# An encoder layer on one core: raw tiles of y in the weight ring, the pooling gate in the attention branch's loop, and the last combinations behind the last token tile's norm

## The chip, the cores and the metric

The kernel runs on one core of one Trainium2 chip. The metric is the device time of one execution, in microseconds (us). The core's engines run side by side, each with its own queue in program order: TensorE (PE) for matmuls and transposes, VectorE (DVE) for arithmetic on tiles, ScalarE (ACT) for activations, copies and casts, GpSimd (POOL) for a part of the arithmetic, and SyncE (SP), which issues most of the transfers (DMAs). They wait for one another through semaphores. Tiles lie in SBUF, 128 partitions of 128 rows or columns, and matmul results in eight banks of PSUM.

## The reference

One layer (DEPTH = 1) of an encoder over 1024 tokens with 1024 channels, in float32:

```python
h = rmsnorm(x, g_mix[l])
z = h @ w_in[l]
...
y_pool = pool_mixer(u_pool, w_pool_grp[l], pool_scale[l])
...
y_attn = diff_attention(q, k, v, g_q[l], g_k[l], lam, g_sub[l], lambda_init)

gates = jax.nn.sigmoid(h @ w_gate[l] + b_gate[l])
merged = (gates[..., :D_MODEL] * (y_pool @ w_branch_pool[l])
          + gates[..., D_MODEL:] * (y_attn @ w_branch_attn[l]))
x = x + merged @ w_out[l]

h2 = rmsnorm(x, g_ffn[l])
x = x + jnp.square(jax.nn.relu(h2 @ w_up[l])) @ w_down[l]
```

`y_attn` ends in a norm per head: a scale per token and head, and a gain `g_sub` per channel. `w_branch_pool` is 512 x 1024, `w_branch_attn` and `w_out` 1024 x 1024, `w_up` 1024 x 4096 and `w_down` 4096 x 1024.

## The kernel before

*How numbers are held.* Each float32 operand of a product is split in a high part (a cast, on ScalarE) and a low part (the difference, on VectorE or GpSimd): `split` (L115). A product is three matmuls, high by high, high by low and low by high: `mm3` (L120, the matmuls at L123 to L125).

*Stages.* After the norm, the projections, the pooling mixer, the attention and the gate products `g` (whose sums are kept in DRAM as `g_dram`), the stages around the change are these, in the order in which TensorE runs them:

1. *Pooling branch* `bp` (`branch_pool` L215, called in the loop L795 to L801). Eight groups `d` of 128 output channels, two halves of 512 tokens each, 12 matmuls per half. `gate` (L204) loads the pooling gate's sums into two tiles `gp` and takes their sigmoid; L220 multiplies the product out of its PSUM bank by it into `mp`. The same loop prepares the attention branch's other operand: `load_split` (L188) loads a raw tile of `y` (128 channels by 1024 tokens, `ryT`), loads the head's scales `rb` as a broadcast row, multiplies the two with the gain (L196), and splits the result into `yT`. The raw tiles come from `raw` (L109), a pool of N_RAW = 2 buffers, which the raw weights use too.
2. *Attention branch* `ba` (loop L803 to L814). For each of the eight groups, `load_cols` (L148) loads a raw tile `rba` of `w_branch_attn` and splits it into two tiles `wba`; a gate tile `ga` is loaded; two halves of 24 matmuls follow; L810 multiplies the bank by `ga`, GpSimd adds `mp` (L811), and the sum is split into `mT`.
3. *Output projection* `op` (`out_proj`), with the residual added on VectorE into the token tile `y[t]`, for eight token tiles of 128 tokens.
4. *Second norm* (`norm_token` L887): the sum of squares `nsq` on ScalarE, the mean and a power on VectorE and GpSimd (`rsq`, the power at L246), the scale on ScalarE (L898), the gain `gfb` on VectorE (L901), eight transposes on TensorE (L904, `hb`). Tokens 4 to 7 go through `second_half` (L959), which makes the operands T1 and T2 of a Strassen-Winograd product; `combine` (L972) makes T3, 22 and T4 of them, and splits T1.
5. *Up projection* (`up_pair` L1012): `w_up` in 16 pairs of column blocks, seven products of 12 matmuls per pair, on operands of the weights (`A`, and the sums S1 to S4, split into `AS`) and of the tokens (B11, B21, T1, T2, T3, 22, T4). The products are gathered in banks called X, Y, Z and W: X takes the first, sixth and seventh product in turn, and its content is copied out by ScalarE in between (x1 L1028, U2 L1055, U3 L1064).
6. *Down projection*, with banks `Da` and `Db`.

*What sets the order.* The tile framework takes the program, orders the instructions of each engine by priority and by what is ready, and puts in the waits. `tc.cur_priority` is set by hand where something is to come earlier or later. A tile of a pool can be written again only when all readers of its former content are done. So the number of buffers of a pool sets how far ahead a load can go. Split weights come out of the ring `wt` (L129): eight slots called W, then four called fw, counted in turn. Small tiles of 512 columns come from `tmp` (two `fr` and two `fo` tiles, in turn).

In the up projection the two lists that the change touches are these. `up_pair` is a generator: its first stretch, up to the first `yield`, makes products 1 and 2, which need only B11 and B21; the second issues a load; the rest makes the other five. The loop at L1091 runs `second_half` for tokens 4 to 7 with priorities of the output projection; the loop at L1096 then advances pairs 0 to 3 and calls `combine` for T1, T3, 22 and T4.

Of the kernel before, what the change touches and what calls it, by code (L numbers as in the profile page):

```python
# [17 lines left out]
P = 128  # L18
# [37 lines left out]
def encoder_kernel(  # L56
# [52 lines left out]
    def raw(shape, name):  # L109
        return rpool.tile(shape, F32, tag="raw", name=name)  # L110

    def f(ap):
        return ap.bitcast(F32)

    def split(hi, lo, src, lo_eng=None):  # L115

        nc.scalar.copy(hi, src)  # L117
        (lo_eng or nc.vector).tensor_tensor(lo, src, f(hi), op=ALU.subtract)  # L118

# [8 lines left out]

    def wt(shape, name):  # L129

        wcount[0] += 1
        if wcount[0] > N_QKVW and (wcount[0] - N_QKVW - 1) % (N_W + N_FW) >= N_W:
            return fw_tile(shape, name)
        return wpool.tile(shape, F32R, tag="W", name=name, bufs=N_W)

    def fw_tile(shape, name):
        return wpool.tile(shape, F32R, tag="fw", name=name, bufs=N_FW)

# [6 lines left out]
    def fu_tile(name):  # L145
        return fq.tile([P, S], F32, tag="fu", name=name)
# [42 lines left out]
    def load_split(src, r0, name, tile_fn, scale=None):  # L189

        rw = raw([P, S], f"r{name}")
        nc.sync.dma_start(rw, src[r0 : r0 + P, :])
        if scale is not None:
            rb, row = scale
            nc.sync.dma_start(rb, row.partition_broadcast(P))
            nc.vector.scalar_tensor_tensor(rw, rw, gs, rb, op0=ALU.mult, op1=ALU.mult)  # L196
        ts = []
        for th in range(2):
            t = tile_fn([P, 2, 512], F32R, f"{name}_{th}", th)
            split(t[:, 0, :], t[:, 1, :], rw[:, th * 512 : (th + 1) * 512])  # L200
            ts.append(t)
        return ts
# [11 lines left out]

    def branch_pool(d, ws, gts, gp, ps_fn):  # L215
        gate(gts, d)
        m = htile([P, S], F32, f"mp{d}", 1)
        for th in range(2):
            ps = proj_T(ps_fn(f"bp{d}_{th}"), ws, lambda k, th: pair(ypT[k][th]), th, nk=4)
            nc.vector.tensor_tensor(m[:, th * 512 : (th + 1) * 512], ps, gp[th], op=ALU.mult)  # L220
        mp.append(m)
# [570 lines left out]
    ypT = [load_split(p_dram, g * P, f"ypT{g}", ypt_tile) for g in range(4)]  # L792
    mp, yT = [], []
    for d in range(NK):
        if d % 2 == 0 and d + 2 < NK:  # L795
            ws_bp[d + 2] = load_cols2(w_branch_pool, (d + 2) * P, f"bp{d + 2}")
        gp = [tmp(f"gp{d}_{th}") for th in range(2)]
        branch_pool(d, ws_bp[d - d % 2][d % 2], [(gp[0], 0, 512), (gp[1], 512, S)], gp, bank)
        rb = fu_tile(f"rb{d}") if d % 2 else ut([P, S], F32, f"rb{d}")
        yT.append(load_split(y_dram, d * P, f"yT{d}", yt_tile(d), (rb, r_dram[d])))  # L800
    mT = {}  # L801
    for d in range(NK):
        ws = load_cols(w_branch_attn, d * P, f"ba{d}")  # L803
        ga = fu_tile(f"ga{d}") if d % 2 else ut([P, S], F32, f"ga{d}")
# [26 lines left out]
    def sub(eng, out_, a, b):  # L831
# [7 lines left out]
    pr2 = [pool_of(hs, "pr20", 1, side="right")]  # L839
    py = pool_of(norms, "py", 4, side="right")  # L840
    nt = pool_of(norms, "nt", 1, side="right")
    Bq = {
        q: tuple(nb_pool.tile([P, 4, 512], F32R, tag="h", name=f"B{q}{i}") for i in "hl")
# [7 lines left out]
    def out_proj(ws, t, dh):  # L851
        th, c0 = t // 4, (t % 4) * P
        cs = slice(dh * 512, (dh + 1) * 512)
        if t not in y:
            y[t] = py.tile([P, D], F32, tag="y", name=f"y{t}")
        nc.sync.dma_start(y[t][:, cs], x[t * P : (t + 1) * P, cs])
# [26 lines left out]
    def b_split(q, c0, src, eng):  # L883
        hi, lo = Bq[q]
        split(hi[:, :, c0 : c0 + P], lo[:, :, c0 : c0 + P], src, eng)

    def norm_token(t, bank_fn):  # L887
# [9 lines left out]
        rsq(rs, rs, 1, 1.0)  # L897
        nc.scalar.activation(yn, yn, AF.Copy, scale=rs)  # L898
        for j, b in enumerate(ps):
# [57 lines left out]
    kept_b = {}  # L957
    T1s = {}

    def second_half(t):  # L960
# [3 lines left out]
        nc.sync.dma_start(t1, nd[0, t - 4])  # L964
        b12, b22 = norm_token(t, lambda j, name: bm.tile([P, 512], F32, tag="ZWY"[j], name=name))
        sub(dve, t1, b12, t1)
# [3 lines left out]
        nc.scalar.copy(kept_b[t][:, 1], b22)  # L970
        b_split("T2", c0, t2, dve)

# [42 lines left out]
    def up_pair(p):  # L1015
# [23 lines left out]
        def store(name, src, queue=nc.sync):  # L1039
# [7 lines left out]
        S1, S2, S3, S4 = (  # L1047
            (e2 if p % 3 or i > 2 else es).tile([P, 4, P], F32, tag="sm", name=f"s{i}_{p}")
            for i in range(1, 5)
# [38 lines left out]
    pairs = [up_pair(p) for p in range(NP)]  # L1088
    now = tc.cur_priority
    for t in range(4, NT):  # L1090
        tc.cur_priority = prio[min(t + 1, NT - 1)]  # L1091
        second_half(t)
    tc.cur_priority = now
    AHEAD = 4
    for p, q in zip(range(AHEAD), ("T1", "T3", "22", "T4")):
        next(pairs[p])  # L1096
        if q == "T1":
            next(pairs[0])
        if q == "T3":
            body = tc.cur_priority  # L1100
        combine(q)
    norms.close()
    e2 = pool_of(hs, "e2", N_E2, side="right")
    pr2.append(pool_of(hs, "pr21", N_R2 - 1, side="right"))
    now, tc.cur_priority = tc.cur_priority, body
    for _ in pairs[0]:
# [184 lines left out]
```

## Time and profile before

| what | before |
|---|---|
| median of 3 runs | 1564.49 us (1564.31 to 1566.15) |
| profiled execution, its own time | 1563.08 us |
| span of that execution in the profile | 1561.3 us |
| mean granted clock of TensorE | 0.997 of full speed |
| instructions in the profile | 22059, of them 7649 matmuls and transposes |

The page of the profile gives, for one execution, the busy time of each engine, the chain of work that ended last, and the costliest groups of instructions. A group's row names the line, the engine, the operation and its output and inputs by the program's names. The list of waits names, for an engine, the tile that it waited to use, the engine, tile and line that released it, the total in us, how often, and the longest. A row of the order of time has the start in us, the length in us, the engine and line, the operation, and in brackets the idle time before it with what ended it; "xN" joins N like instructions that follow one another. A row of a view by tile has the shortest, median and longest duration in ns, and the first and last start. A row of a stretch has its length, then the busy time and the number of instructions of PE, its weight loads, DVE, ACT and POOL, the granted clock of TensorE (1.00 is full speed), the DMA engines' busy share and GB/s.

### The profile page before, as it was taken

How to read it: one execution, taken by the hardware profiler on the slowest of the kernel's cores; microseconds unless marked ns; L12 is line 12 of the kernel's file. 1: busy time of each engine (PE TensorE's matmuls, PEld its weight loads, DVE VectorE, ACT ScalarE, POOL GpSimd, SP SyncE). 2: the span in 40 equal slices, each digit the busy share in tenths (PEclk: the TensorE clock that was granted, in tenths of full speed). 3: DMA queues.
4: the chain of work that ended last, by engine and by line, in shares of the span. 5: the costliest groups of instructions: out<-in, count | busy, mean ns of one | idle time of the engine just before them, and what ended most of it. 6: DMA issues, size and time to landing. Idle time of an engine off the chain costs nothing.

```text
span 1561.3 us, 22059 instructions
## 1 busy us (share of the span) xinstructions
PE 1537.9 (99%) x7649; PEld 1323.7 (85%) x7649; DVE 1007.5 (65%) x2273; ACT 809.2 (52%) x1792; POOL 353.3 (23%) x447
## 2 busy tenths in 40 slices
PE   7999999999999999999899999999999999999999
PEld 6999999999999989888788887888888788888887
DVE  7777677777878797645222458766666668556662
ACT  6656656656565655554422556555555634333331
POOL 6433333343434252221644400000000000000000
PEclk9999999999999999999999999999999999999999
DMA  7111212121212021248526634555342789537750
GB/s 228 51 52 48 64 46 63 32 66 49 63 41 70 31 92 42 69 148 283 180 92 184 207 108 121 175 168 177 132 138 108 255 309 382 199 122 248 227 192 27
DMA packets 166393, 206.41 MB, mean 132 GB/s; under 512 B 10037, under 2 KB 102922, under 8 KB 166282
## 3 DMA queue, kind: packets, MB, share of 16 engines
q1 hardware_dynamic: 148874, 177.71, 35.0%
q10 hardware_dynamic: 17408, 27.30, 4.7%
q8 instruction: 60, 0.98, 0.3%
q14 instruction: 51, 0.42, 0.1%
HBM read 150.42 MB, written 54.56 MB: 131 GB/s over the span
## 4 chain that ended last, share of the span: by engine, by line
PE 87%; DVE 4%; DMA 4%; ACT 1%; POOL 1%; issue 1%; SPq 1%; POOLq 0%; DVEq 0%; ACTq 0%
PE z L123 5%; PE z L125 5%; PE z L124 5%; PE Da L124 4%; PE Da L123 4%; PE Da L125 4%; PE g L124 3%; PE g L123 3%; PE g L125 3%; PE Db L124 3%; PE Db L123 3%; PE Db L125 3%; PE X L123 3%; PE X L124 3%; PE X L125 3%; PE sc L496 2%
## 5 line engine op out<-in xcount | busy, mean ns | idle before, releaser
L123 PE MATMUL z<-wqkv,hT 128*128 128x384 f32 x512 | 174.7, 342 | 0.4 <-DVE qn L438 0.3
L125 PE MATMUL z<-wqkv,hT 128*128 128x384 f32 x512 | 174.3, 341 | 0.3 <-DVE hT L118 0.2
L124 PE MATMUL z<-wqkv,hT 128*128 128x384 f32 x512 | 173.6, 339 | 0.0
L507 ACT ACTIVATE s<-s,nm 128x256 f32<-128x256 f32 (+7 forms) x128 | 99.6, 778 | 48.7 <-DVE nm L499 43.3
L246 POOL TENSOR_TENSOR ms<-ms,mhalf 128x4 f32<-128x4 f32 x64 | 66.5, 1040 | 157.6 <-DVE ms L245 139.0
L125 PE MATMUL g<-hT,fwgate 128*128 128x512 f32 x256 | 101.0, 394 | 0.0
L124 PE MATMUL g<-hT,fwgate 128*128 128x512 f32 x256 | 100.9, 394 | 0.0
L123 PE MATMUL g<-hT,fwgate 128*128 128x512 f32 x256 | 100.9, 395 | 0.0
L123 PEld LDWEIGHTS z<-wqkv,hT 128*128 128x128 f32 x512 | 96.8, 189 | 4.3 <-DVE qn L438 1.2
L124 PEld LDWEIGHTS z<-wqkv,hT 128*128 128x128 f32 x512 | 96.8, 189 | 2.9
L125 PEld LDWEIGHTS z<-wqkv,hT 128*128 128x128 f32 x512 | 96.6, 189 | 2.9 <-DVE hT L118 1.3
L499 DVE CUSTOM_DVE_ANT_0 s<-sc,dist 128x512 f32<-128x512 f32 (+3 forms) x128 | 74.7, 586 | 22.1 <-PE sc L497 20.7
L118 POOL TENSOR_TENSOR wqkv<-rqkv,wqkv 128x384 fp32r<-128x384 f32 x60 | 63.8, 1080 | 20.2 <-ACT wqkv L117 18.3
L118 DVE TENSOR_TENSOR AS<-s,AS 128x512 fp32r<-128x512 f32 x64 | 43.9, 688 | 36.9 <-ACT AS L117 36.6
L496 PE MATMUL sc<-K,Q 128*128 128x512 f32 (+2 forms) x192 | 67.2, 355 | 0.1
L497 PE MATMUL sc<-K,Q 128*128 128x512 f32 (+2 forms) x192 | 66.5, 354 | 0.0
L444 POOL TENSOR_TENSOR qn<-qn,ggh 128x128 f32<-128x128 f32 x64 | 32.9, 514 | 137.5 <-DVE qn L438 119.3
L470 ACT CAST Q<-tk 64x128 fp32r<-64x128 f32 x128 | 33.2, 259 | 58.3 <-DVE Q L469 56.5
L467 ACT CAST Q<-tk 64x128 fp32r<-64x128 f32 x128 | 33.1, 258 | 50.5 <-DVE K L466 49.1
L118 POOL TENSOR_TENSOR fwgate<-frgate,fwgate 128x512 fp32r<-128x512 f32 x32 | 45.1, 1412 | 51.9 <-ACT fwgate L117 51.7
L125 PEld LDWEIGHTS g<-hT,fwgate 128*128 128x128 f32 x256 | 48.1, 188 | 8.6
L123 PE MATMUL ba<-yT,wba 128*128 128x512 f32 x128 | 51.2, 400 | 3.9 <-ACT wba L117 3.9
(428 smaller groups left out, 4638.5 us busy)
## 6 DMA issues: line engine op xcount, KB each, us to landing
wd<-in_w_down_dram SPq DMA_DIRECT2D x56, 512.0 KB, 5.8
wu<-in_w_up_dram SPq DMA_DIRECT2D x32, 512.0 KB, 4.5
udS<-us SPq DMA_DIRECT2D x64, 256.0 KB, 2.2
ur<-udS SPq DMA_DIRECT2D x32, 512.0 KB, 3.4
rqkv<-in_w_in_dram SPq DMA_DIRECT2D x64, 192.0 KB, 2.8
ud<-u ACTq DMA_DIRECT2D x48, 256.0 KB, 2.5
ur<-ud SPq DMA_DIRECT2D x24, 512.0 KB, 4.3
frgate<-in_w_gate_dram SPq DMA_DIRECT2D x32, 256.0 KB, 2.9
```

Of the source, the lines that this page charges most:

```text
L118: (lo_eng or nc.vector).tensor_tensor(lo, src, f(hi), op=ALU.subtract)
L123: nc.tensor.matmul(ps, lhs_hi, rhs_hi, start=first, stop=False, **kw)
L124: nc.tensor.matmul(ps, lhs_hi, rhs_lo, start=False, stop=False, **kw)
L125: nc.tensor.matmul(ps, lhs_lo, rhs_hi, start=False, stop=last, **kw)
L246: nc.gpsimd.tensor_tensor(dst, dst, mhalf[:, :n], op=ALU.pow)
L444: nc.gpsimd.tensor_tensor(qn[:, 2:4, :], qn[:, 2:4, :], ggh.unsqueeze(1).broadcast_to([P, 2, HD]), op=ALU.mult)
L467: nc.scalar.copy(q_hi, q)
L470: nc.scalar.copy(Q[other, m, 1, :], q)
L496: nc.tensor.matmul(dst, Q[:, i, 0, :], rhs, start=True, stop=False)
L497: nc.tensor.matmul(dst, Q[:, i, 1, :], rhs, start=False, stop=True)
L499: nc.vector.tensor_tensor_reduce(out=s[i][:, c : c + w], in0=sc[:, 0:w], in1=dist[:, o0 + c : o0 + c + w], scale=2.0 ** -(h + 1), scalar=B ...
L507: nc.scalar.activation(s[i][:, 0:n], s[i][:, 0:n], AF.Exp, bias=last, scale=-1.0, accum_out=Z[:, i, t : t + 1])
```

## The change

The change has these parts.

- `load_split` takes the raw tile from the weight ring `wt`, in F32, where a scale is given (the tiles of `y`); `wt` and `fw_tile` take a type for it. The scales come as a list of tiles: one of 1024 columns as before, or two of 512 from `tmp`, with a load and a multiplication each. Two of every four groups use the halves.
- `branch_pool` no longer loads the gate and no longer multiplies: ScalarE copies the bank into `mp`. The gate's load, sigmoid and multiplication, now in place on `mp`, go into the attention branch's loop.
- The attention branch's weights are loaded ahead: groups 0, 1 and 2 in the pooling loop at d = 5, 6, 7, and group d + 2 at the head of each turn of the attention loop. Group 2 is loaded in both.
- The token tiles `y` come from four pools of one tile each in place of one pool of four, and the pool `nt` is made before them. The pool `e2` of six tiles becomes `e20` (two) and `e21` (four): pair 0 and the pairs divisible by three use `es` and `e20`, pair 1 too, and the others `e21`.
- For the last token tile the second half's sum of squares uses bank Z in place of Y. Pair 0's first two stretches and pair 1's first are advanced before the last token tile's `second_half`, at a priority 100 later than what was reached.
- `combine` of T3, 22 and T4 is put behind the scale of token tile 7 (`issue_after`: what is emitted in that context is not ordered ahead of that instruction), and T4 also behind the split of that tile's T2. `split` and `b_split` return their last instruction for this, and `norm_token` keeps the scale in `scaled`.

```diff
--- before.py
+++ after.py
@@ -115,7 +115,7 @@
     def split(hi, lo, src, lo_eng=None):
 
         nc.scalar.copy(hi, src)
-        (lo_eng or nc.vector).tensor_tensor(lo, src, f(hi), op=ALU.subtract)
+        return (lo_eng or nc.vector).tensor_tensor(lo, src, f(hi), op=ALU.subtract)
 
     def mm3(ps, lhs_hi, lhs_lo, rhs_hi, rhs_lo, first, last, more=False):
 
@@ -126,15 +126,15 @@
 
     wcount = [0]
 
-    def wt(shape, name):
+    def wt(shape, name, dt=F32R):
 
         wcount[0] += 1
         if wcount[0] > N_QKVW and (wcount[0] - N_QKVW - 1) % (N_W + N_FW) >= N_W:
-            return fw_tile(shape, name)
-        return wpool.tile(shape, F32R, tag="W", name=name, bufs=N_W)
-
-    def fw_tile(shape, name):
-        return wpool.tile(shape, F32R, tag="fw", name=name, bufs=N_FW)
+            return fw_tile(shape, name, dt)
+        return wpool.tile(shape, dt, tag="W", name=name, bufs=N_W)
+
+    def fw_tile(shape, name, dt=F32R):
+        return wpool.tile(shape, dt, tag="fw", name=name, bufs=N_FW)
 
     def fo_tile(name):
         return fp.tile([P, 528], F32, tag="fo", name=name, bufs=N_FO)
@@ -188,12 +188,15 @@
 
     def load_split(src, r0, name, tile_fn, scale=None):
 
-        rw = raw([P, S], f"r{name}")
+        rw = raw([P, S], f"r{name}") if scale is None else wt([P, S], f"r{name}", F32)
         nc.sync.dma_start(rw, src[r0 : r0 + P, :])
         if scale is not None:
-            rb, row = scale
-            nc.sync.dma_start(rb, row.partition_broadcast(P))
-            nc.vector.scalar_tensor_tensor(rw, rw, gs, rb, op0=ALU.mult, op1=ALU.mult)
+            rbs, row = scale
+            n = S // len(rbs)
+            for i, rb in enumerate(rbs):
+                js = slice(i * n, (i + 1) * n)
+                nc.sync.dma_start(rb, row[js].partition_broadcast(P))
+                nc.vector.scalar_tensor_tensor(rw[:, js], rw[:, js], gs, rb, op0=ALU.mult, op1=ALU.mult)
         ts = []
         for th in range(2):
             t = tile_fn([P, 2, 512], F32R, f"{name}_{th}", th)
@@ -212,12 +215,12 @@
     def pair(t):
         return t[:, 0, :], t[:, 1, :]
 
-    def branch_pool(d, ws, gts, gp, ps_fn):
-        gate(gts, d)
+    def branch_pool(d, ws, ps_fn):
+
         m = htile([P, S], F32, f"mp{d}", 1)
         for th in range(2):
             ps = proj_T(ps_fn(f"bp{d}_{th}"), ws, lambda k, th: pair(ypT[k][th]), th, nk=4)
-            nc.vector.tensor_tensor(m[:, th * 512 : (th + 1) * 512], ps, gp[th], op=ALU.mult)
+            nc.scalar.copy(m[:, th * 512 : (th + 1) * 512], ps)
         mp.append(m)
 
 
@@ -790,17 +793,30 @@
 
     ws_bp = {0: load_cols2(w_branch_pool, 0, "bp0")}
     ypT = [load_split(p_dram, g * P, f"ypT{g}", ypt_tile) for g in range(4)]
-    mp, yT = [], []
+    mp, yT, ws_ba = [], [], {}
+
     for d in range(NK):
         if d % 2 == 0 and d + 2 < NK:
             ws_bp[d + 2] = load_cols2(w_branch_pool, (d + 2) * P, f"bp{d + 2}")
-        gp = [tmp(f"gp{d}_{th}") for th in range(2)]
-        branch_pool(d, ws_bp[d - d % 2][d % 2], [(gp[0], 0, 512), (gp[1], 512, S)], gp, bank)
-        rb = fu_tile(f"rb{d}") if d % 2 else ut([P, S], F32, f"rb{d}")
+        elif d > NK - 4:
+            j = len(ws_ba)
+            ws_ba[j] = load_cols(w_branch_attn, j * P, f"ba{j}")
+        branch_pool(d, ws_bp[d - d % 2][d % 2], bank)
+        if d % 4 < 2:
+            rb = [fu_tile(f"rb{d}") if d % 2 else ut([P, S], F32, f"rb{d}")]
+        else:
+            rb = [tmp(f"rb{d}_{i}") for i in range(2)]
         yT.append(load_split(y_dram, d * P, f"yT{d}", yt_tile(d), (rb, r_dram[d])))
     mT = {}
     for d in range(NK):
-        ws = load_cols(w_branch_attn, d * P, f"ba{d}")
+        if d + 2 < NK:
+            ws_ba[d + 2] = load_cols(w_branch_attn, (d + 2) * P, f"ba{d + 2}")
+        ws = ws_ba.pop(d)
+        gp = [tmp(f"gp{d}_{th}") for th in range(2)]
+        gate([(gp[0], 0, 512), (gp[1], 512, S)], d)
+        for th in range(2):
+            mh = mp[d][:, th * 512 : (th + 1) * 512]
+            nc.vector.tensor_tensor(mh, mh, gp[th], op=ALU.mult)
         ga = fu_tile(f"ga{d}") if d % 2 else ut([P, S], F32, f"ga{d}")
         gate(whole(ga)[0], NK + d)
         for th in range(2):
@@ -837,8 +853,8 @@
     nb_pool = pool_of(hs, "nb", 4, side="right")
     pr1 = pool_of(hs, "pr1", N_R1, side="right")
     pr2 = [pool_of(hs, "pr20", 1, side="right")]
-    py = pool_of(norms, "py", 4, side="right")
     nt = pool_of(norms, "nt", 1, side="right")
+    py = [pool_of(norms, f"py{i}", 1, side="right") for i in range(4)]
     Bq = {
         q: tuple(nb_pool.tile([P, 4, 512], F32R, tag="h", name=f"B{q}{i}") for i in "hl")
         for q in ("11", "21")
@@ -852,7 +868,7 @@
         th, c0 = t // 4, (t % 4) * P
         cs = slice(dh * 512, (dh + 1) * 512)
         if t not in y:
-            y[t] = py.tile([P, D], F32, tag="y", name=f"y{t}")
+            y[t] = py[t % 4].tile([P, D], F32, tag="y", name=f"y{t}")
         nc.sync.dma_start(y[t][:, cs], x[t * P : (t + 1) * P, cs])
         if th:
             ps = pb.tile([P, 512], F32, tag="b", name=f"op{t}_{dh}")
@@ -882,7 +898,9 @@
 
     def b_split(q, c0, src, eng):
         hi, lo = Bq[q]
-        split(hi[:, :, c0 : c0 + P], lo[:, :, c0 : c0 + P], src, eng)
+        return split(hi[:, :, c0 : c0 + P], lo[:, :, c0 : c0 + P], src, eng)
+
+    scaled = {}
 
     def norm_token(t, bank_fn):
 
@@ -895,7 +913,7 @@
         ps = [bank_fn(j, f"hb{t}_{j}") for j in range(2)]
         nc.vector.tensor_scalar(rs, ss[:, 0:1], ss[:, 1:2], 1.0 / D, op0=ALU.add, op1=ALU.mult)
         rsq(rs, rs, 1, 1.0)
-        nc.scalar.activation(yn, yn, AF.Copy, scale=rs)
+        scaled[t] = nc.scalar.activation(yn, yn, AF.Copy, scale=rs)
         for j, b in enumerate(ps):
             js = slice(j * 512, (j + 1) * 512)
             nc.vector.tensor_tensor(yn[:, js], yn[:, js], gfb[:, js], op=ALU.mult)
@@ -955,20 +973,20 @@
         Bq[q] = tuple(hpT[q].tile([P, 4, 512], F32R, tag="h", name=f"B{q}{i}") for i in "hl")
 
     kept_b = {}
-    T1s = {}
+    T1s, T2_made = {}, {}
 
     def second_half(t):
         c0 = (t - 4) * P
         t1, t2 = (ev(f"{n}_{t}", (P, 4, P)) for n in ("t1", "t2"))
         T1s[t] = t1
         nc.sync.dma_start(t1, nd[0, t - 4])
-        b12, b22 = norm_token(t, lambda j, name: bm.tile([P, 512], F32, tag="ZWY"[j], name=name))
+        b12, b22 = norm_token(t, lambda j, name: bm.tile([P, 512], F32, tag=("ZWY" if t < NT - 1 else "ZWZ")[j], name=name))
         sub(dve, t1, b12, t1)
         sub(dve, t2, b22, t1)
         kept_b[t] = y[t].rearrange("p (q a b) -> p q a b", q=2, a=4)
         nc.scalar.copy(kept_b[t][:, 0], b12)
         nc.scalar.copy(kept_b[t][:, 1], b22)
-        b_split("T2", c0, t2, dve)
+        T2_made[t] = b_split("T2", c0, t2, dve)
 
     def combine(q):
         for t in range(4, NT):
@@ -1045,7 +1063,9 @@
         A.update(load(1, pr2[p % 3 > 0]))
         yield
         S1, S2, S3, S4 = (
-            (e2 if p % 3 or i > 2 else es).tile([P, 4, P], F32, tag="sm", name=f"s{i}_{p}")
+            (e2[1] if p % 3 and p != 1 else e2[0] if i > 2 else es).tile(
+                [P, 4, P], F32, tag="sm", name=f"s{i}_{p}"
+            )
             for i in range(1, 5)
         )
         add(dve, S1, A["21"], A["22"])
@@ -1086,22 +1106,35 @@
         store("S4", s4)
 
     pairs = [up_pair(p) for p in range(NP)]
-    now = tc.cur_priority
+    now = tc.cur_priority + 100
+
+
     for t in range(4, NT):
+        if t == NT - 1:
+            tc.cur_priority = now
+            for p in (0, 0, 1):
+                next(pairs[p])
+            now = tc.cur_priority
         tc.cur_priority = prio[min(t + 1, NT - 1)]
         second_half(t)
     tc.cur_priority = now
     AHEAD = 4
-    for p, q in zip(range(AHEAD), ("T1", "T3", "22", "T4")):
-        next(pairs[p])
-        if q == "T1":
-            next(pairs[0])
+    for p, q in enumerate(("T1", "T3", "22", "T4")):
+        if p > 1:
+            next(pairs[p])
         if q == "T3":
             body = tc.cur_priority
-        combine(q)
+
+        with ExitStack() as later:
+            if p:
+                later.enter_context(tc.issue_after(scaled[NT - 1].ins))
+            if q == "T4":
+                later.enter_context(tc.issue_after(T2_made[NT - 1].ins))
+            combine(q)
     norms.close()
-    e2 = pool_of(hs, "e2", N_E2, side="right")
+    e2 = [pool_of(hs, "e20", 2, side="right")]
     pr2.append(pool_of(hs, "pr21", N_R2 - 1, side="right"))
+    e2.append(pool_of(hs, "e21", N_E2 - 2, side="right"))
     now, tc.cur_priority = tc.cur_priority, body
     for _ in pairs[0]:
         pass
```

## The prediction

> **What bounds the kernel now.** I read the page's head and chain of waits first, then the list of what TensorE waited for, then the stretches of 20 us around those waits, and last the order of time on each engine there.
>
> ```profile
> span 1561.3 us, 22059 instructions
> ...
> PE 1537.9 (99%) x7649; PEld 1323.7 (85%) x7649; DVE 1007.5 (65%) x2273; ACT 809.2 (52%) x1792; POOL 353.3 (23%) x447
> ...
> PE 87%; DVE 4%; DMA 4%; ACT 1%; POOL 1%; issue 1%; SPq 1%; POOLq 0%; DVEq 0%; ACTq 0%
> ...
> PE hps L272 <- DVE hn L267: 9.0, 1, 9.0
> PE ba L123 <- ACT wba L117: 3.9, 1, 3.9
> PE Z L123 <- ACT BT1h L117: 2.8, 1, 2.8
> PE X L123 <- ACT U L1055: 1.5, 1, 1.5
> ...
> 740.00:760.00 20.00, 15.92 (x63) 12.15 (x62) 7.55 (x11) 8.99 (x14) 7.62 (x6) 0.91 0.65 211
> ...
> 940.00:960.00 20.00, 17.24 (x66) 13.19 (x65) 16.08 (x28) 11.93 (x22) 3.87 (x1) 0.84 0.17 44
> ...
> 1240.00:1260.00 20.00, 18.50 (x81) 14.87 (x80) 16.67 (x20) 10.67 (x15) 0.00 (x0) 1.00 0.87 319
> ```
>
> TensorE (PE) is busy for all but 23.4 us of the span, and the change leaves its matmuls as they are. So the change can only give back idle time of PE, and the slow matmuls behind it. The wait of 9.0 stands at the head, which the change does not touch. What can be won lies in three places: the first attention-branch product `ba` (3.9), the first product on the last token (`Z`, 2.8), and a product of the last pair (`X`, 1.5). In each of the three stretches (columns: length, busy us of PE, weight load, DVE, ACT, POOL, then the granted clock) PE is short of 20 by just that wait. In the first two the clock is below 1 as well.
>
> **The first wait.** PE, then SyncE, VectorE, ScalarE and GpSimd in order of time, then the tile gp (min, median and max in ns, and us from issue to landing):
>
> ```profile
> 744.37 0.39 PE L125 MATMUL bp<-ypT,wbp 128*128 128x512 f32 x1
> 748.71 0.80 PE L123 MATMUL ba<-yT,wba 128*128 128x512 f32 x1 [3.95 <-ACT wba L117]
> ...
> 752.24 0.39 PE L124 MATMUL ba<-yT,wba 128*128 128x512 f32 x1
> 752.47 0.39 PE L125 MATMUL ba<-yT,wba 128*128 128x512 f32 x1
> ...
> 739.41 0.32 SPq L192 DMA_DIRECT2D ryT<-y_dram x1
> ...
> 741.21 0.38 SPq L151 DMA_DIRECT2D rba<-in_w_branch_attn_dram x1
> ...
> 744.15 1.28 DVE L196 SCALAR_TENSOR_TENSOR ryT<-ryT,gs,rb 128x1024 f32<-128x1024 f32 x1 [2.37 <-issue]
> ...
> 748.04 1.14 ACT L117 CAST wba<-rba 128x512 fp32r<-128x512 f32 x2 [1.21 <-DMA rba<-in_w_branch_attn_dram]
> ...
> 748.73 2.53 POOL L118 TENSOR_TENSOR wba<-rba,wba 128x512 fp32r<-128x512 f32 x2 [19.00 <-ACT wba L117]
> ...
> L206 SPq DMA_DIRECT2D gp<-g_dram x16: 319/329/497, 674.9 to 741.8; - x16
> L207 ACT ACTIVATE gp<-gp,zero x16: 708/723/733, 679.4 to 749.1; 128x512 f32<-128x512 f32 x16
> L220 DVE TENSOR_TENSOR mp<-bp,gp x16: 677/684/692, 706.6 to 749.8; 128x512 f32<-128x512 f32 x16
> ...
> DMA to landing us min/median/max: 5.0/5.9/6.4
> ```
>
> The weights are fetched only at 741.21, because eight y tiles go through two raw buffers ahead of them, the last leaving at 739.41; they are cast at 748.04. PE stands for 3.95. From 752.24 on its matmuls start 0.23 apart, but the seven steps from 748.71 to 752.24 take 3.53 where 1.61 would do, 1.9 more. The place costs 5.9.
>
> **The second wait.** Token 7's norm: the power on GpSimd, the scale, the product, the transposes, and what follows:
>
> ```profile
> L246 POOL TENSOR_TENSOR nrs<-nrs,mhalf x8: 548/550/3872, 873.1 to 944.5; 128x1 f32<-128x1 f32 x8
> ...
> 944.53 3.87 POOL L246 TENSOR_TENSOR nrs<-nrs,mhalf 128x1 f32<-128x1 f32 x1 [20.29 <-DVE nrs L245]
> ...
> 948.43 1.15 ACT L898 ACTIVATE y<-y,nrs 128x1024 f32<-128x1024 f32 x1 [4.06 <-POOL nrs L246]
> ...
> 949.62 1.29 DVE L901 TENSOR_TENSOR y<-y,gfb 128x512 f32<-128x512 f32 x2 [1.63 <-ACT y L898]
> ...
> 950.46 1.23 PE L904 MATMUL hb<-identf,y 128*128 128x128 f32 x8
> ...
> 953.41 0.68 DVE L832 TENSOR_TENSOR t<-hb,t 128x512 f32<-128x512 f32 x1
> ...
> 953.77 0.63 ACT L117 CAST BT1h<-t 128x512 fp32r<-128x512 f32 x1
> ...
> 954.45 0.80 PE L123 MATMUL Z<-BT1h,AS 128*128 128x512 f32 x1 [2.76 <-ACT BT1h L117]
> 955.04 0.63 PE L123 MATMUL Y<-B21h,A 128*128 128x512 f32 x1
> 955.47 0.63 PE L124 MATMUL Y<-B21l,A 128*128 128x512 f32 x1
> ...
> 960.45 0.40 PE L125 MATMUL Z<-BT1h,AS 128*128 128x512 f32 x1
> ```
>
> VectorE, at 16.08 of 20 in this stretch, runs subtractions of the combinations between the steps of the norm, and the power lasts 3.87 against 0.55 for the other seven tokens. After the transposes (done at 951.69) PE waits 2.76, and its matmuls come at 0.43 (955.04 to 955.47) in place of 0.23: from 954.45 to 960.45 there are 14 steps, 6.00 where 3.22 would do, 2.8 more. The place costs 5.6.
>
> **The third wait.**
>
> ```profile
> 1241.67 1.04 ACT L117 CAST w_1h<-wd 128x1024 fp32r<-128x1024 f32 x1
> 1242.62 1.04 ACT L117 CAST w_2h<-wd 128x1024 fp32r<-128x1024 f32 x1
> 1243.56 0.58 ACT L1055 COPY U<-X 128x512 f32<-128x512 f32 x1
> ...
> 1244.19 0.50 PE L123 MATMUL X<-BT3h,AS 128*128 128x512 f32 x1 [1.50 <-ACT U L1055]
> 1244.53 0.40 PE L124 MATMUL X<-BT3l,AS 128*128 128x512 f32 x1
> ```
>
> The copy of `X` stands behind casts of the down weights on ScalarE. No slow matmuls follow this gap. It costs 1.5.
>
> **The change part by part.**
>
> *Raw tiles and early weights.* The y tiles take eight slots of the weight ring in place of two raw buffers. In the new order SyncE issues four ryT back to back, then the first `rba` right behind the fetch of bp6, released by GpSimd's subtraction for bp4. `bp` is 16 groups of 12 matmuls at 0.23, 44 us, so it begins at 700.5, and that fetch leaves some 4 us later, landing by 711 at the slowest rate above (6.4). The last y tile waits for the end of bp3, halfway, at 722.5. With 6.4 to land, 1.28 to scale, two casts and two subtractions (under 4), it is ready by 734. That is 10 us before `ba` begins. So the 3.95 goes, and without the gap the 1.9 as well: -5.9. From below: a wait remains only if that load takes 10 us longer, and then the whole 5.9 does. What is issued beside it: four more fetches of r in halves, four half multiplies in place of two whole ones, and one fetch of ba2 (two casts, two subtractions of 1.27 on GpSimd) that is made twice. GpSimd's row above shows 19.00 idle just there, which is the cover; were it gone, 2.53.
>
> *Gate moved.* The 16 evacuations go from VectorE (684 ns) to copies on ScalarE (0.58, as the copy at 1243.56), and 16 in-place multiplies follow later. ScalarE works 8.99 of 20 there, so the copies hide; PE has eight banks, and a copy may be some 20 us late. What could wait is the later part. The gates pass one pair at a time through two tiles: fetch 5.9, sigmoid 0.72, multiply 0.68, 7.3 a round. From about 729 (the scaling of the last y tile frees the tiles) the sixth round ends at 773. VectorE's first evacuation of `ba` is queued behind it, and with it GpSimd's additions. PE needs that bank after eight groups of 24 matmuls of 0.23, that is 44 us after 744.6, at 788.8. ScalarE's copies of bp6 and bp7 and its casts of wba5 stand behind sigmoids of the same rounds; wba5 is cast near 780 and needed at 800. SyncE's wba7 is queued behind the seventh, near 781, and needed at 821. Slack 16: nil. It is gone if a round takes 9.9, which the slowest fetch (6.4, a round of 7.8) is far from.
>
> *Last token.* In the new order the combinations of all but T1 stand behind token 7's scale on VectorE and ScalarE. Only a few operations are left between its steps: the power starts about 942.9 for 944.53 and lasts its usual 0.55, and the scale (1.15) and the product (two of some 0.7) are done about 946.4. The transposes now stand behind 75 matmuls after token 6's, 950.7, so that even a power of 3.87 (product at 949.7) would be in time. Behind them come 21 matmuls, 4.9 us, that need nothing of token 7; the first `Z` is due at 956.6. The subtraction and the cast for it (0.68 and 0.63) sit behind the copies of the other half, at 955.3, 1.3 early. That takes off 2.76 and 2.8. But what was late elsewhere moves here: pair 0's third product on `X` now follows its second with nothing between, so PE must wait for ScalarE's copy of `X` (U2), which is queued behind three casts of BT4h (0.6 each): about 963.7 where PE is there at 962.2. The nearest row is the same wait at the last pair, 1.50; I take 1.6, between 0 (casts done early) and 1.6 + 2.8 (if the clock drops). The next pair's S2 hangs on a wu load behind it: 0.6, between 0 and 1.5. Sum of the place: -5.6 + 1.6 + 0.6 = -3.4, between -5.6 and 0.
>
> *Last pair.* In the new order the copy of `X` has two casts of 1.04 fewer ahead of it: ready 2.1 earlier, 1.50 late before. So -1.5; at worst the loads of w, issued earlier, hold something else by as much: 0.
>
> *Pools.* Four pools for y, and e2 split in two and four tiles, only change who waits for whom (below).
>
> **A rule beside the second row.** The row at 955.04 to 955.47 shows half rate after a gap of 2.76, and that at 1244.53 none after 1.50. The Trainium skill, "TensorE: Matmul & The Clock Gate", Part 1: The HAM clock gate, says that the clock halves after an idle window of about 3.4 us. By it the gap of 2.76 would have cost itself alone, and the sum would be 2.8 smaller, 1556.5. The trace has the slow steps, so it decides, and the sum stands.
>
> **The sum.** -5.9 - 3.4 - 1.5 = -10.8. The profiled execution took 1563.1 (the span and 1.8 around it): 1552.3. The median of the runs is 1.4 higher, so 1553.7.
>
> **The rivals.**
> (a) *The last token still keeps PE waiting.* The margin at `Z` is 1.3, and the low half of BT1 hangs on a cast that waits for a load. Then the place gives nothing, or the new waits take the 5.6 back: 1557.1. For it: margins under 2 us in a row of five steps. Against: 21 matmuls of cover that were not there.
> (b) *The change does not do what it says for the weights*: `rba` is held by its slot or a load until after 740. Then 5.9 stays: 1559.6. Against it: the 10 us.
> (c) *Slower: the S tiles.* Pairs 2, 4, 5, 7, 8 and so on now share four tiles where six were shared, so the sums of one pair wait for the splits of the pair before. Place: VectorE, eight times from pair 4 on. From the split of S1 three products (12 x 0.23 each, 8.3 us) run before the next pair's; the chain sum, difference, cast, subtraction takes 2.7. It decides once VectorE, at 17.9 us of 20 in its busiest stretch, lags over 5.6 us. Price 1.5 (the X row) to 5.6 (the Z place) each; at 2.8 (its wait alone) 22 us: 1576. Against: VectorE is 65% busy, and no wait of a pair but the last is in the list.
>
> ```profile
> 960.00:980.00 20.00, 20.00 (x88) 16.41 (x88) 17.91 (x30) 11.33 (x21) 0.00 (x0) 0.99 0.75 220
> ```
>
> **How the numbers follow.** Forecast 0.58, (a) 0.22, (b) 0.09, (c) 0.11. The time is that of the forecast, 1553.7. Its own bounds are 1551.5 (no new wait: -13.0) and 1556.5 (the new wait drops the clock); the range takes in (a) and (b) and stops short of (c): 1551 to 1560. A measurement tells 0.2%, 3.1 us, from no change. Forecast, (a) and most of (b) lie below 1561.4: faster 0.84; same 0.06, a (b) and (a) together (1563.0) or a mild (c); slower 0.10, the rest of (c).
>
> **What would show it.** Right: `ba <- wba` is gone from the list of PE's waits and the stretch 740 to 760 has 20.0 at clock 1.0; the power of token 7 lasts near 0.55; a wait `X <- U` of about 1.6 near 960 in place of `Z <- BT1h`; none at the last pair. Wrong: waits of `ba` on VectorE or wba near 790 (gate rounds of 10 us), a row of waits on AS2 through the pairs (c), or a wait at BT1l.

## The result and the profile after

| what | before | after |
|---|---|---|
| median of four runs | 1564.43 us (1564.31 to 1566.15) | 1553.80 us (1553.41 to 1555.37) |
| span of the profiled execution | 1561.3 us | 1551.6 us |

The ratio is 0.9931 (95% interval 0.9914 to 0.9949): 0.7% faster, and 0.1 us from the 1553.7 predicted. That is closer than the steps deserve, as will be seen.

The list of TensorE's waits after the change, in the columns of the one before:

```profile
PE hps L275 <- DVE hn L270: 8.8, 1, 8.8
PE X L123 <- ACT U L1075: 2.0, 2, 1.3
PE ta L555 <- DVE AT_0l L118: 1.0, 1, 1.0
PE ta L555 <- DVE AT_4l L118: 0.6, 1, 0.6
PE X L125 <- DVE AS L118: 0.6, 1, 0.6
...
PE bp L123 <- ACT rT L613: 0.2, 1, 0.2
```

`ba` on wba and `Z` on BT1 are gone. A wait of `X` on the copy U is there twice, 1.3 and 0.7, and 0.6 on AS. The stretches, in the same columns as before (the eighth number is the granted clock):

```profile
740.00:760.00 20.00, 20.00 (x88) 16.24 (x87) 6.22 (x8) 9.94 (x18) 6.64 (x5) 1.00 0.62 191
...
940.00:960.00 20.00, 19.32 (x89) 15.47 (x88) 18.58 (x31) 15.52 (x30) 0.00 (x0) 1.00 0.49 159
960.00:980.00 20.00, 19.39 (x86) 15.72 (x85) 18.53 (x31) 11.00 (x21) 0.00 (x0) 1.00 0.59 170
...
1220.00:1240.00 20.00, 18.69 (x83) 15.16 (x82) 16.24 (x21) 14.69 (x21) 0.00 (x0) 1.00 0.89 319
```

The first place is full and at full clock. The second is short by 0.7 and 0.6 in place of 2.8, and the clock no longer drops. The third is still short by 1.3, some 10 us earlier than before. TensorE's order of time at the three remaining gaps:

```profile
957.75 0.50 PE L123 MATMUL X<-BT3h,AS 128*128 128x512 f32 x1 [0.68 <-ACT U L1075]
...
967.72 0.50 PE L125 MATMUL X<-BT2h,AS 128*128 128x512 f32 x1 [0.61 <-DVE AS L118]
...
1234.54 0.50 PE L123 MATMUL X<-BT3h,AS 128*128 128x512 f32 x1 [1.31 <-ACT U L1075]
```

Each of these costs its gap and 0.1 (the next matmul starts 0.34 later, for 0.23). To find where the time came from, the span is cut by the first matmul of a stage, from the views by tile: `bp` (L123) begins at 701.0 in both, `op` at 839.8 before and 834.7 after, `Da` at 1249.8 and 1240.1.

| stretch | before | after | difference | predicted |
|---|---|---|---|---|
| from the first `bp` to the first `op` | 138.8 | 133.7 | -5.1 | -5.9 |
| from the first `op` to the first `Da` | 410.0 | 405.4 | -4.6 | -3.4 - 1.5 = -4.9 |
| from the first `Da` to the end | 311.5 | 311.5 | 0 | 0 |

In the first stretch the gap of 3.95 and the slow matmuls behind it (those that start 0.43 and more apart in place of 0.23) are gone. `bp` takes 0.5 longer (44.1, from 701.0 to 745.12, for 43.6), of which 0.2 is the wait on rT, and `ba` some 0.3. In the second, the last token gave more than forecast and the last pair almost nothing.

### The profile page after: what moved, and what is told of

The parts are those of the page before. It is cut to its first block, busy times and chain, and to the rows that moved or that the text cites. A ratio compares the mean times of both kernels' runs of the same rounds, so it can differ in the third digit from the quotient of the medians.

```text
span 1551.6 us, 22088 instructions
## 1 busy us (share of the span) xinstructions
PE 1533.6 (99%) x7649; PEld 1320.8 (85%) x7649; DVE 1011.3 (65%) x2277; ACT 816.7 (53%) x1810; POOL 354.8 (23%) x449
## 4 chain that ended last, share of the span: by engine, by line
PE 89%; DVE 4%; DMA 3%; ACT 1%; issue 1%; POOL 1%; SPq 0%; ACTq 0%; POOLq 0%; DVEq 0%
PE z L125 5%; PE z L123 5%; PE z L124 5%; PE Da L124 4%; PE Da L123 4%; PE Da L125 4%; PE g L123 3%; PE g L124 3%; PE g L125 3%; PE Db L124 3%; PE Db L123 3%; PE Db L125 3%; PE X L125 2%; PE X L123 2%; PE X L124 2%; PE sc L499 2%
## 5 line engine op out<-in xcount | busy, mean ns | idle before, releaser
L123 PE MATMUL z<-wqkv,hT 128*128 128x384 f32 x512 | 174.7, 342 | 0.4 <-DVE qn L441 0.3
L510 ACT ACTIVATE s<-s,nm 128x256 f32<-128x256 f32 (+7 forms) x128 | 99.6, 778 | 49.2 <-DVE nm L502 44.1
L123 PE MATMUL g<-hT,fwgate 128*128 128x512 f32 x256 | 100.9, 395 | 0.0
L123 PEld LDWEIGHTS z<-wqkv,hT 128*128 128x128 f32 x512 | 96.9, 189 | 4.2 <-DVE qn L441 1.0
L125 PEld LDWEIGHTS g<-hT,fwgate 128*128 128x128 f32 x256 | 48.1, 188 | 8.6
L123 PEld LDWEIGHTS g<-hT,fwgate 128*128 128x128 f32 x256 | 48.2, 188 | 7.1
```

The costliest lines, as they stand in the source:

```text
L123: nc.tensor.matmul(ps, lhs_hi, rhs_hi, start=first, stop=False, **kw)
L125: nc.tensor.matmul(ps, lhs_lo, rhs_hi, start=False, stop=last, **kw)
L510: nc.scalar.activation(s[i][:, 0:n], s[i][:, 0:n], AF.Exp, bias=last, scale=-1.0, accum_out=Z[:, i, t : t + 1])
```

## The experiments

All are the changed kernel with some of its parts undone, and each ran once. They were profiled on other chips, where the time up to `bp` differed by up to 1.5 us (701.0 here, 702.5 in one run). So they are compared by the first two stretches of the table above, called A (from the first `bp` to the first `op`) and B (from there to the first `Da`).

| kernel | first `bp` | A | B | span |
|---|---|---|---|---|
| before | 701.0 | 138.8 | 410.0 | 1561.3 |
| changed | 701.0 | 133.7 | 405.4 | 1551.6 |
| `first_half` | 702.1 | 133.9 | 410.0 | 1557.6 |
| `last_half` | 702.5 | 140.3 | 407.7 | 1562.0 |
| `gate_back` | 701.7 | 141.0 | 405.5 | 1559.7 |
| `no_early` | 700.8 | 133.9 | 406.2 | 1552.5 |
| `raw_back` | 701.5 | 144.7 | 406.1 | 1563.8 |
| `gate_only` | 701.1 | 134.4 | 407.6 | 1554.7 |
| `ring_only` | 701.1 | 140.6 | 405.4 | 1558.7 |
| `no_queue` | 701.6 | 133.8 | 410.1 | 1557.0 |
| `no_advance` | 702.1 | 133.4 | 412.6 | 1559.6 |
| `e2_whole` | 701.0 | 133.3 | 408.9 | 1554.7 |
| `py_whole` | 701.3 | 133.6 | 406.9 | 1553.3 |
| `own_tile` | 701.3 | 134.3 | 403.8 | 1551.9 |

Where the first half of the change stands whole, A is 133.3 to 134.3. Where the second half does, B is 405.4 to 406.2, and 407.6 and 407.7 in the two runs (`gate_only`, `last_half`) whose wait in the last pair, 1.93 and 1.99, had nine slow matmuls behind it. Differences as small as these ranges are not told apart.

**The two halves alone.** `first_half` has the changes down to the attention branch, `last_half` those behind it.

> The kernel before with the first parts of the change alone: y's raw tiles in the weight ring, the gate and the early weights; token tiles and combinations as before. Theory (the parts add up): the wait of ba on wba is gone and the output projection begins 5.1 us earlier than before, as in the changed kernel (834.7 for 839.8); the waits of Z (2.8) and of the last X (1.5) stay; span about 1556.2. Rival (the token tile's gain hangs on the first part, since it starts earlier and finds its loads landed): a span other than 1556.2 by more than 0.7, with a wait of Z other than 2.8.

> The kernel before with the other parts alone: pools of y, e2 in two, pairs advanced, combinations queued. Theory (the parts add up): the wait of ba (3.9) stays, that of Z is gone, a wait of X on U of about 0.7 in pair 0 and of 1.3 in the last pair; span about 1561.3 - 4.6 = 1556.7. Rival: the wait of Z stays in part (over 1 us), span over 1558.

Measured: `first_half` A 133.9, B 410.0, the waits as the theory has them (`Z` 2.8, the last `X` 1.6); the span of 1557.6 was 1.4 over the forecast, 1.1 of it ahead of `bp`. `last_half` A 140.3, B 407.7, the wait of `Z` gone, span 1562.0. The waits of each half come and go without the other, as the theory says, but the span of the second was 5 us over the forecast. Its start was 1.5 later; the unchanged wait for wba was followed by 12 slow matmuls in place of 6; and its wait on U in the last pair was 1.99, followed by slow matmuls, of which more below.

**The parts of the first half.** `gate_back` puts the gate back into the pooling loop:

```diff
-    def branch_pool(d, ws, ps_fn):
+    def branch_pool(d, ws, gts, gp, ps_fn):
+        gate(gts, d)
...
-            nc.scalar.copy(m[:, th * 512 : (th + 1) * 512], ps)
+            nc.vector.tensor_tensor(m[:, th * 512 : (th + 1) * 512], ps, gp[th], op=ALU.mult)
...
```

> The changed kernel with the gate's load, sigmoid and multiplication back in the pooling loop, in place of ScalarE's copies. Theory (the first wait hung on the raw tiles and the late weights alone): no wait of ba, span within 0.7 of 1551.6. Rival (the gate's transfers on SyncE and its multiplications ahead of the y tiles held the weights): ba waits 1 to 4 us, span 1552.6 to 1557.5.

Measured: A 141.0, more than before the change, and a span of 1559.7, beyond the rival's 1557.5 too. The theory failed. The rival's waits came, but on yT and not on the weights, and one of `bp` was new:

```profile
PE ba L124 <- DVE yT L118: 2.4, 2, 1.7
...
PE ba L123 <- ACT yT L117: 1.6, 1, 1.6
PE bp L123 <- DVE mp L223: 1.5, 1, 1.5
```

`no_early` drops the early weights:

```diff
-        elif d > NK - 4:
-            j = len(ws_ba)
-            ws_ba[j] = load_cols(w_branch_attn, j * P, f"ba{j}")
...
-        if d + 2 < NK:
-            ws_ba[d + 2] = load_cols(w_branch_attn, (d + 2) * P, f"ba{d + 2}")
-        ws = ws_ba.pop(d)
+        ws = load_cols(w_branch_attn, d * P, f"ba{d}")
```

> The changed kernel with each group's attention weights loaded at the head of its own turn, once, none in the pooling loop. Theory (two raw buffers are what held them, and these are free now): the first load is still issued well before the stage's end, ba waits under 0.5, span within 0.7 of 1551.6. Rival (the place in the program holds it): ba waits 2 us or more on wba, and with the slow matmuls behind it the span is 1554 to 1557.5.

Measured: A 133.9 and no wait of `ba`: the early weights, and the second load of ba2, neither bring nor cost anything that shows here (the span of 1552.5 is 0.9 over the changed kernel's, 0.8 of it in B). `raw_back` puts the y tiles back in two buffers:

```diff
-        rw = raw([P, S], f"r{name}") if scale is None else wt([P, S], f"r{name}", F32)
+        rw = raw([P, S], f"r{name}")
```

> The changed kernel with y's raw tiles back in the two raw buffers; gate and early weights stay as changed. Theory (two buffers for eight tiles and the weights are the cause): SyncE issues the y tiles two at a time again, the first attention weights share these buffers, and ba waits 2 us or more on wba or yT; span 1554 to 1558. Rival (early weights alone do it): no wait of ba, span within 0.7 of 1551.6.

Measured: A 144.7 and a span of 1563.8, beyond the theory's 1558, with a wait of 7.2 for yT:

```profile
PE ba L123 <- ACT yT L117: 7.2, 1, 7.2
...
749.35 0.38 SPq L151 DMA_DIRECT2D rba<-in_w_branch_attn_dram  x1
750.30 0.32 SPq L192 DMA_DIRECT2D ryT<-y_dram  x1
```

The early weights now take turns with the y tiles in the two buffers, and the last y tile leaves only at 750.30. So this run does not tell what the two buffers cost by themselves, and the ring and the gate's move were run each alone, without early weights.

> The changed kernel with y's raw tiles back in the two raw buffers and each group's attention weights loaded once, at the head of its turn: of the first part only the gate's move is left (and r in halves). Theory (ring and gate's move are needed together): ba waits at least 2 us, from the first bp to the first op it takes over 137 (133.7 in the changed kernel, 138.9 before). Rival (raw_back was slow only because the early weights took the two buffers; the gate's move alone does it): no wait of ba over 0.5, 133.5 to 134.5 for that stretch.

> The changed kernel with the gate back in the pooling loop and each group's attention weights loaded once, at the head of its turn: of the first part only the raw tiles in the ring are left. Theory (ring and gate's move are needed together, the gate's transfers and multiplications hold the y tiles): ba waits for yT or wba by 2 us or more, the stretch from the first bp to the first op over 137. Rival (gate_back was slow only because the early weights' loads took SyncE and the bandwidth from the y tiles): no wait over 0.5, 133.5 to 134.5.

Measured: `gate_only` A 134.4, `ring_only` A 140.6. The rival of the first expectation held (but for one wait of 0.62 on GpSimd's wba): the gate's move alone, with r in halves, gives 4.4 of the 5.1. Of the second the theory held: `ba` waits for yT, and the ring, with r in halves, makes A 1.8 longer than before. (`gate_only` joins the edits of `raw_back` and `no_early`, `ring_only` those of `gate_back` and `no_early`. Both keep r in halves; no run has it whole.) First `gate_only`, the order of time on SyncE and on ScalarE:

```profile
737.77 0.32 SPq L192 DMA_DIRECT2D ryT<-y_dram  x1
738.98 0.38 SPq L151 DMA_DIRECT2D rba<-in_w_branch_attn_dram  x1
...
744.24 1.14 ACT L117 CAST wba<-rba 128x512 fp32r<-128x512 f32 x2 [0.90 <-DMA rba<-in_w_branch_attn_dram]
```

With the same two buffers the last y tile leaves 1.6 us earlier than before (739.41) and the weights 2.2 earlier (741.21). They are cast 3.8 earlier (748.04), so they also land faster. The stretch from 740 to 750 (the last but one number is the DMA engines' busy share), in `gate_only` and in the kernel before:

```profile
740.00:750.00 10.00, 9.34 (x40) 7.07 (x39) 6.46 (x8) 6.23 (x12) 2.99 (x2) 1.00 0.62 194
```

```profile
740.00:750.00 10.00, 5.98 (x24) 4.10 (x22) 6.33 (x10) 5.39 (x8) 1.27 (x2) 0.93 0.85 288
```

The DMA engines are busy 0.62 for 0.85. From 702 to 742 SyncE sends fourteen of the gate's transfers of 256 KB (`gp`) in the kernel before, and three in `gate_only`; that the weights land faster for this reason is likely, but no run shows it by itself. The gate held VectorE too. The weights wait for a raw buffer that a subtraction for yT frees, and before the change two of the gate's multiplications (L220) stand among the operations that lead to it:

```profile
736.12 0.69 DVE L220 TENSOR_TENSOR mp<-bp,gp 128x512 f32<-128x512 f32 x1
...
739.30 0.68 DVE L220 TENSOR_TENSOR mp<-bp,gp 128x512 f32<-128x512 f32 x1
739.90 1.28 DVE L118 TENSOR_TENSOR yT<-ryT,yT 128x512 fp32r<-128x512 f32 x2
```

From the scaling of a y tile (734.92) to the end of that subtraction it took 6.3 before, and 5.1 in `gate_only` (from 733.90). So of the 3.8, 1.2 is time of VectorE, 1.0 is that y tile arriving earlier, and 1.6 the weights landing faster. Now `ring_only`, the order of time on VectorE and on SyncE:

```profile
746.72 3.34 DVE L199 SCALAR_TENSOR_TENSOR ryT<-ryT,gs,rb 128x512 f32<-128x512 f32 x2 [4.59 <-DMA rb<-r_dram]
...
752.28 0.75 DVE L199 SCALAR_TENSOR_TENSOR ryT<-ryT,gs,rb 128x512 f32<-128x512 f32 x1 [1.01 <-DMA rb<-r_dram]
...
739.98 1.94 SPq L198 DMA_DIRECT2D rb<-r_dram  x2
...
748.38 0.32 SPq L198 DMA_DIRECT2D rb<-r_dram  x1
...
750.10 0.32 SPq L198 DMA_DIRECT2D rb<-r_dram  x1
```

The y tiles have long been there, but the halves of r that they are scaled by are issued as late as 750.10. These halves come from `tmp`, the four small tiles that the gate uses too, and each waits for one to come free: by the trace the last two were released by a scaling (L199) of a half before them, others by a multiplication of the gate (L223; one at 723.2). In the whole change, where the gate comes to `tmp` only behind them, the last half leaves by 721.

**The parts of the second half.** `no_queue` no longer puts the combinations behind token 7's scale and split:

```diff
-            if p:
-                later.enter_context(tc.issue_after(scaled[NT - 1].ins))
-            if q == "T4":
-                later.enter_context(tc.issue_after(T2_made[NT - 1].ins))
```

> The changed kernel with the combinations not put behind token 7's scale and split; the pairs are still advanced first. Theory (it is the 21 matmuls of cover that take the wait at Z away, and queueing only gives the margin): the power of token 7 on GpSimd lasts longer than 0.55 again, Z waits under 1.5, span 1551.6 to 1553.5. Rival (the queueing does it): Z waits 2 to 3 us with slow matmuls behind, span 1555 to 1557.5.

Measured: B 410.1, the whole gain gone, as the rival has it, with two waits of `Z` (4.0 in all, and 1.7 in slow matmuls behind them). TensorE's order of time in `no_queue`, and GpSimd's power:

```profile
953.87 0.50 PE L123 MATMUL Z<-BT1h,AS 128*128 128x512 f32 x1 [1.54 <-ACT BT1h L117]
956.88 0.50 PE L124 MATMUL Z<-BT1l,AS 128*128 128x512 f32 x1 [2.51 <-DVE BT1l L118]
...
945.49 0.86 POOL L249 TENSOR_TENSOR nrs<-nrs,mhalf 128x1 f32<-128x1 f32 x1 [25.70 <-DVE nrs L248]
```

`no_advance` advances the pairs only after the last token tile's norm, as before the change:

```diff
-        if t == NT - 1:
-            tc.cur_priority = now
-            for p in (0, 0, 1):
-                next(pairs[p])
-            now = tc.cur_priority
...
```

> The changed kernel with the pairs advanced where they were, after the last token tile's norm; combinations still queued behind its scale. Theory (cover): with fewer matmuls behind the transposes Z waits 1 to 3 us for BT1, span 1553 to 1556. Rival (queueing alone is enough, since the norm ends some 5 us earlier): no wait of Z, span within 0.7 of 1551.6.

Measured: B 412.6, slower than before: `Z` waits 3.03 for BT1, and pair 1 twice for AS (1.63 and 1.57), more than the theory's 1 to 3; the span, 1559.6, lies beyond its 1556. Neither edit is enough without the other, though the expectations had set the one against the other. The two pools: `e2_whole` makes e2 one pool of six again:

```diff
-            (e2[1] if p % 3 and p != 1 else e2[0] if i > 2 else es).tile(
+            (e2[0] if p % 3 or i > 2 else es).tile(
...
-    e2 = [pool_of(hs, "e20", 2, side="right")]
+    e2 = [pool_of(hs, "e20", N_E2, side="right")]
...
```

> The changed kernel with e2 as one pool of six again. Theory (four tiles are enough for the S sums of neighbouring pairs, the split costs nothing): the waits of the pairs are those of the changed kernel (0.7 and 0.6 in pairs 0 and 1, 1.3 to 2.1 in the last), and from the first op to the first Da it takes 405.4, plus or minus 0.9. Rival (the split is paid in the pairs or in the last one): over 1 us less than 405.4. Third way (the pool of six is free only later, and the pairs' sums with it): over 406.5, with a wait on AS.

`py_whole` makes y one pool of four again:

```diff
-    py = [pool_of(norms, f"py{i}", 1, side="right") for i in range(4)]
+    py = pool_of(norms, "py", 4, side="right")
...
-            y[t] = py[t % 4].tile([P, D], F32, tag="y", name=f"y{t}")
+            y[t] = py.tile([P, D], F32, tag="y", name=f"y{t}")
```

> The changed kernel with the token tiles y in one pool of four again. Theory (a tile can be written when its own readers are done, in one pool as in four): 405.4, plus or minus 0.9, from the first op to the first Da. Rival (with one pool the room is given back only as a whole, so what the pairs put there, e20 and the raw tile of the next load, comes later): a wait on AS in pair 0 or 1 that is over 1.5, and 406.5 or more.

Measured: `e2_whole` B 408.9, `py_whole` 406.9. The third way and the rival held. From their lists of waits, first e2 whole, then y whole:

```profile
PE X L123 <- ACT AS L117: 2.2, 1, 2.2
PE X L123 <- ACT U L1075: 2.1, 2, 1.5
PE X L125 <- DVE AS L118: 1.0, 1, 1.0
```

```profile
PE X L123 <- ACT U L1075: 2.3, 2, 1.6
PE X L125 <- DVE AS L118: 1.6, 1, 1.6
```

With e2 whole, the sums `s` of pair 0 that come from it run on VectorE at 956.18, in the changed kernel at 942.59, and AS is late by 3.2 in all, against 0.6. With y whole AS is late by 1.6. That rival is less sure: B is 0.7 above the 406.2 that a kernel with the pools split reached (`no_early`, AS late by 1.0). No wait of the later pairs shows in any of the lists.

**The last pair.** The order of time on ScalarE in the changed kernel shows what the copy U waited for:

```profile
1226.91 0.85 ACTq L1058 DMA_DIRECT2D ud<-u  x2
...
1230.95 1.05 ACT L117 CAST w_0h<-wd 128x1024 fp32r<-128x1024 f32 x1
1233.90 0.59 ACT L1075 COPY U<-X 128x512 f32<-128x512 f32 x1 [1.91 <-DMA ud<-u]
```

The casts are done at 1232.0; then ScalarE stands for 1.91, until the store of u22 of the pair before, issued at 1226.91, has landed and frees the tile that U2 is to be written in. `own_tile` gives it another:

```diff
-        U2 = ev(f"U2_{p}")
+        U2 = ev(f"U2_{p}") if p < NP - 1 else e2[1].tile([P, 512], F32, tag="sm", name=f"U2_{p}")
```

> The changed kernel with one edit: in the last pair the copy U2 goes to a tile of e21, which no store holds, in place of the ring of nine that u22 of the pair before was stored from. Theory (the copy waits 1.91 for that store to land, while ScalarE's casts are done): the wait of X on U in the last pair falls from 1.3 to under 0.2, span 1551.6 - 1.5 = 1550.1. Rival (ScalarE's casts of the down weights hold it, as before the change): the wait stays over 1, span within 0.4 of 1551.6.

Measured: the wait is gone (only the 0.7 of pair 0 is left in the list), and B is 403.8, 1.6 less. But the span is 1551.9 for the 1550.1 expected. From the first `Da` to the end it takes 312.5 in place of 311.5, with a new wait in its list,

```profile
PE Db L123 <- ACT w_0h L117: 0.4, 1, 0.4
```

and A was 134.3 in that run. So the cause of the wait is shown; the gain is mostly given back, and none of these kernels beats the changed one by what a measurement can tell.

## Why the prediction was right, and where not

*What bounds the kernel.* Right: the gain is idle time of TensorE at two of the three places, with the slow matmuls behind it.

*First wait: -5.9 for the raw tiles and the early weights, nil for the gate.* The size was near (-5.1), the attribution wrong. The order forecast did come: the first weights leave at 705.66, and the last y tile is ready at 738.1, 7 us ahead of `ba` for the 10 forecast. But the gate's move, costed at nil with its cover, gives 4.4 without that order, and without its move the ring and the early weights, with r in halves, gain nothing (`gate_back`). The size follows from the gap, whatever closes it; that it was closed hung on a part that was costed at nil, and that is luck. The prediction asked what hides the gate's work in its new place, and that held: no wait of `ba` near 790, and the gate's rounds were shorter than forecast, the last sigmoid at 774.8 and the gate's loads landing in 3.1 (median) for 5.9. It did not ask what the gate had held in its old place: VectorE's time, DMA time and, once r comes in halves, the `tmp` tiles. With the gate moved, the early weights are worth nothing that shows, and the ring without them at most the 0.5 between `gate_only` and `no_early`; the early weights do need the ring (`raw_back`). Whether the ring and the early weights would have been enough with the gate in its old place and r whole was not run. Read from the trace of before, the wait of `ba` was put down to the two buffers because the last y tile left late; the gate's multiplications on VectorE and the load on the DMA engines beside it (0.85) had been left unread.

*Last token: -5.6 + 1.6 + 0.6.* The first term held: the row

```profile
937.66 0.55 POOL L249 TENSOR_TENSOR nrs<-nrs,mhalf 128x1 f32<-128x1 f32 x1 [18.60 <-DVE nrs L248]
```

is 5.2 earlier than the forecast of 942.9, just what the stage before had given, and 0.55 long. So is the first `Z`, at 951.45 without a gap for the 956.6 forecast, behind 21 matmuls that need nothing of token 7. The 0.6 on AS was 0.61. The 1.6 was 0.68: the casts of BT4h, which were to be queued ahead of the copy, were done, and ScalarE waited for the product. What is left is the length of the copy. That the queueing and the advanced pairs do it together is shown by `no_queue` and `no_advance`. The pools, counted at nothing, are part of it: with e2 whole B is 3.5 longer; with y whole it is 1.5 longer, which these single runs hardly tell from nothing.

*Last pair: -1.5.* This term failed. "In the new order the copy of `X` has two casts of 1.04 fewer ahead of it" was true, but a second wait stood behind the first, for the store that frees the tile, and 1.3 was left (-0.2 in all). The bound of 0 that the prediction kept had another reason, the loads of w.

*The total.* -5.1 - 4.6 is -9.7 for -10.8 forecast. The median lay 0.4 above the profiled execution (1553.41) and not 1.4 as before; the two errors cancel to 0.1, which is luck too.

*Rivals.* (a) did not come about, but shows how near it was: without either of two edits the place gives nothing. (b) did not come about; in `gate_back`, `raw_back` and `ring_only`, with one part or two undone, `ba` waits, but for yT. (c) is refuted by the lists, which have no wait of a pair between pair 1 and the last; the split of e2 even gains.

## What to carry to other kernels

When work is moved off a stage, ask not only what covers it where it goes, but what it held where it was: tiles, a place in an engine's queue, a share of the DMA engines. A wait that is removed uncovers the next one of the same instruction, so look up every release of it, also the store that frees the tile it writes. Parts of a change should be tried alone before one of them is given the credit.

## What the runs showed of the hardware

The slow matmuls behind a gap do not follow from its length. The same wait for wba had 6 slow steps behind it before (3.95; 1.9 us lost) and 12 in `last_half` (3.85; 3.1 lost). In the last pair a gap of 1.99 was followed by them, in `last_half`,

```profile
1243.28 0.50 PE L123 MATMUL X<-BT3h,AS 128*128 128x512 f32 x1 [1.99 <-ACT U L1059]
1243.62 0.40 PE L124 MATMUL X<-BT3l,AS 128*128 128x512 f32 x1
...
1244.45 0.63 PE L124 MATMUL X<-BT3l,AS 128*128 128x512 f32 x1
1244.88 0.63 PE L125 MATMUL X<-BT3h,AS 128*128 128x512 f32 x1
```

and one of 2.07 was not, in `raw_back`:

```profile
1246.72 0.50 PE L123 MATMUL X<-BT3h,AS 128*128 128x512 f32 x1 [2.07 <-ACT U L1075]
...
1248.22 0.40 PE L123 MATMUL X<-BT3h,AS 128*128 128x512 f32 x1
1248.45 0.39 PE L124 MATMUL X<-BT3l,AS 128*128 128x512 f32 x1
```

In `no_advance` a gap of 3.03 had two slow steps behind it. Lone gaps up to 1.65 never had more than the first step slow; two of about that length, 2.3 us apart, had nine slow steps behind the second (`no_advance`, 1.63 and 1.57). The Trainium skill, "TensorE: Matmul & The Clock Gate", Part 1: The HAM clock gate, calls the window free-running and the count of slow matmuls at a kernel's start run-variable, and the varying counts here are like that; its about 3.4 us of idleness is not needed here, as 1.99 and 2.76 show. So the 2.8 that the prediction counted for slow matmuls behind `Z` (the same in `first_half`, behind 2.77) could not be had from the length of the gap: behind gaps of 1.9 to 4 us the loss was 0.1 to 3.1 here. What decides it is not shown.
